# First products, output projection and last norm of a two-layer trunk rearranged between the engines

## Chip, cores and metric

The kernel runs on one core of a Trainium2 chip. The metric is the device time of one execution in microseconds (us), as the median of several runs. The engines are named as in the profile: PE (matmuls), DVE (vector), ACT (activations, casts), POOL, and SP, which issues most loads.

## What is computed

A trunk of two layers on a sequence of T = 1024 tokens with D = 1024 features, batch 1, float32. Layer 0 mixes tokens with a gated linear recurrence (Griffin), layer 1 with a causal pooling mixer; behind each stands an MLP with squared ReLU and 4096 hidden units. Each sub-layer is fed by an RMS norm whose scale and shift come from a conditioning vector c through a large weight matrix (w_mod), and a final RMS norm ends it.

```
for i in range(DEPTH):                         # DEPTH = 2
    mod = silu(c) @ w_mod[i] + b_mod[i]        # 6 columns of D
    sh_m, sc_m, gt_m, sh_f, sc_f, gt_f = split(mod, 6)
    h = rms_norm(x, norm_mix_g[i]) * (1 + sc_m) + sh_m
    y = recurrent_mixer(h, ...) if i == 0 else pool_mixer(h, ...)
    x = x + gt_m * y
    h = rms_norm(x, norm_ffn_g[i]) * (1 + sc_f) + sh_f
    u = relu(h @ ffn_w1[i])
    x = x + gt_f * ((u * u) @ ffn_w2[i])
return rms_norm(x, final_norm_g)

# recurrent_mixer:
#   gate = gelu(h @ w_y + b_y);  xr = conv4(h @ w_in + b_in)
#   r, g = sigmoid(block-diagonal products of xr);  a = exp(c * r * log_sigmoid(lam))
#   s = scan(a, sqrt(1 - a*a) * g * xr);            y = (s * gate) @ w_out + b_out
```

## The kernel before

**Layout.** Everything is kept transposed: features on the 128 partitions in 8 blocks, tokens along the free axis in two halves h = 0 and 1 of 512. x, h and all products are tiles of 128x512.

**Products.** Each float32 product is made of three fp32r matmuls (`mm3`, lines 188 to 190): high part of the weight by high part of the data, high by low, low by high. Eight blocks of features are accumulated, so one output tile takes 24 matmuls. The data are split in `norm_split` (line 291; high part `hh` by ACT, low part `hl` by DVE). A weight of 128x1024 is loaded by SP into a buffer of a pool of three (`rawp`), cast by ACT (line 180) and subtracted by DVE or POOL (line 181), in two halves of 512 (`split_unit`, `split_part`). With "dma" it goes another way (`neg_part`, lines 163 to 165): ACT casts, ACT negates the cast, and a DMA issued by POOL loads the weight a second time and adds it to the negated cast.

**Conditioning.** A column of `mod` is made from eight rows of w_mod: a load of 512 KB into a `rawp` buffer (`mb`) and a DVE multiply with accumulation (line 207). `mod_steps` lists these steps; `drip(n)` puts n of them into the program, and `split_unit` calls it `rate[0]` times behind each weight load. The first two columns (scale and shift of the first norm) are different: their rows `mw` have buffers of their own, and a custom DVE operation (line 333) works on them during the first products.

**First products (lines 316 to 413).** `w_in` for output blocks 0 to 5 and half 0, run with the feature block k on the outside, so that 6 accumulators grow while k proceeds: 18 matmuls (line 410) for each k. For each k, DVE makes the two columns of k (`bias_of`, `scale_of`), xn = x * rstd is made by DVE (k = 0) or POOL (`normed`), ACT makes `hh` and the unsplit value, and DVE the low part. `prepare(q)` splits the weights w_k of q = 0 to 3 (each serves k = 2q and 2q + 1): three casts on ACT, three subtractions on POOL (q = 0: on DVE). `after()` writes out the order of ACT, DVE and POOL by hand here: each call stands behind the one before on its engine.

**Recurrence (lines 565 to 577).** For each of four heads `hd` and each half: `gates` (cast of the conv output into `xchl`, line 516; 24 short matmul steps; sigmoid, exp, tanh, sqrt on ACT; scan on DVE), and two `gelu_block`s with 24 matmuls each. At the end the result is split into `yh`, `yl` (`split_y`, line 558).

**Output projection (lines 586 to 607).** 16 tiles of 24 matmuls, weights w_o0 to 3 for both halves, then 4 to 7. ACT scales (line 602), DVE adds to x (line 603), ACT squares and DVE or POOL adds the square to a sum (`SumSq`, line 243; each letter of the plan names the engine of a step, and each engine of a plan has a part of its own). When half 0 is done and one more tile is under way, `ffn_norm` runs: `rstd_bcast` (line 266) sums each part over partitions with matmuls of one column (line 272), takes root and reciprocal, and spreads the result with two matmuls (line 286).

**MLPs, pooling and end.** The MLP goes in 8 chunks of hidden units (`f1`, `f2`); the first chunk of layer 0 follows the output projection. The last chunk of layer 1 runs half 0, then tokens 0 to 255 and 256 to 511 of half 1 (`last_chunk`), and each is followed by its `final_norm`.

Within the limits of pools and dependencies, the order on an engine is set by a scheduler by priority, in the order in which the program is written, except where `after()` sets it.

## Time and profile before

| | |
|---|---|
| median of 3 runs | 1766.14 us (1762.34 to 1766.17) |
| the profiled execution | 1766.89 us, span 1765.1 us |
| mean granted PE clock | 0.984 of full speed |
| PE / DVE / ACT / POOL busy | 97% / 77% / 54% / 31% of the span |
| DMA over the span | 102 GB/s |

The span is the time from the first to the last record; 1.8 us of the execution lie around it. A busy PE says little alone, since matmuls at a low clock also count as busy. What a stretch loses is seen from PE's waits in it, and from the granted clock: the fraction of full speed, of which there are two levels, 1.2 GHz (0.5) and 2.4 GHz (1.0). DVE, ACT and POOL cost time only where PE waits for them.

### The profile page before, as it was taken

The numbers are of one execution on the slowest core, as the hardware profiler recorded it, in microseconds if no ns is written. First come the engines' busy times: TensorE is split into PE (matmuls) and PEld (weight loads), VectorE is DVE, ScalarE is ACT, GpSimd is POOL, SyncE is SP. The second block draws the span as 40 slices with busy tenths as digits, with TensorE's granted clock in tenths as the row PEclk, the third lists the DMA queues.
The fourth block names the chain that finished last, engine by engine and source line by source line (L and its number), as shares of the span: only waits on it lengthen the run. The fifth ranks groups of instructions, "written<-read, shape, count | busy, mean of one in ns | idle before, by whom it ended". The sixth has DMA issues, their size and how long they took to land.

```text
span 1765.1 us, 20959 instructions
## 1 busy us (share of the span) xinstructions
PE 1704.2 (97%) x7510; PEld 1397.7 (79%) x7510; DVE 1367.9 (77%) x2092; ACT 959.7 (54%) x1648; POOL 544.3 (31%) x442
## 2 busy tenths in 40 slices
PE   5899989989999999999999999999999999999997
PEld 3687768778788888888888888888878787878787
DVE  8898866678888888888874698649786968686836
ACT  4578884346354545444456688745444454545432
POOL 4323332151313223241407433312231404140403
PEclk8999999989999999999999999999999999999998
DMA  9223413521424142423217889861111111111202
GB/s 354 90 72 107 144 60 108 190 84 48 140 71 135 60 143 72 132 73 118 84 48 166 196 182 194 171 167 47 61 37 60 54 42 60 48 61 36 78 7 96
DMA packets 59577, 180.80 MB, mean 102 GB/s; under 512 B 6352, under 2 KB 8784, under 8 KB 59472
## 3 DMA queue, kind: packets, MB, share of 16 engines
q1 hardware_dynamic: 47376, 157.43, 27.7%
q0 software_dynamic: 12096, 22.03, 7.5%
q8 instruction: 59, 0.97, 0.2%
q14 instruction: 46, 0.38, 0.1%
HBM read 175.24 MB, written 4.19 MB: 102 GB/s over the span
## 4 chain that ended last, share of the span: by engine, by line
PE 71%; DVE 15%; ACT 5%; DMA 4%; issue 3%; POOL 1%; SPq 0%; DVEq 0%; ACTq 0%; POOLq 0%
PE mm L188 23%; PE mm L189 23%; PE mm L190 23%; DMA mb<-in_wmod 3%; DVE mb L207 2%; DVE mw L333 1%; DVE xca L449 1%; DVE xa L780 1%; PE sm L272 1%; DVE xb L780 1%; POOL xa L789 1%; DVE xcb L449 1%; DVE hl L301 1%; DVE nt L294 1%; POOL asq L538 1%
## 5 line engine op out<-in xcount | busy, mean ns | idle before, releaser
L188 PE MATMUL mm<-hh,w_w 128*128 128x512 f32 x1024 | 400.3, 391 | 1.0 <-DVE xa L780 1.0
L189 PE MATMUL mm<-hl,w_w 128*128 128x512 f32 x1024 | 399.4, 390 | 0.0
L190 PE MATMUL mm<-hh,w_w 128*128 128x512 f32 x1024 | 399.3, 390 | 0.0
L789 POOL TENSOR_TENSOR xb<-xb,c 128x512 f32<-128x512 f32 x104 | 149.8, 1440 | 603.9 <-ACT c L784 558.9
L188 PEld LDWEIGHTS mm<-hh,w_w 128*128 128x128 f32 x1024 | 192.8, 188 | 42.5 <-DVE xa L780 2.7
L190 PEld LDWEIGHTS mm<-hh,w_w 128*128 128x128 f32 x1024 | 192.8, 188 | 40.4
L189 PEld LDWEIGHTS mm<-hl,w_w 128*128 128x128 f32 x1024 | 192.8, 188 | 39.8
L789 POOL TENSOR_TENSOR xa<-xa,c 128x512 f32<-128x512 f32 x104 | 160.0, 1538 | 145.0 <-ACT c L784 145.0
L784 ACT ACTIVATE c<-c,mod 128x512 f32<-128x512 f32 x104 | 75.3, 724 | 204.5 <-DVE c L810 119.0
L207 DVE SCALAR_TENSOR_TENSOR mb<-mb,cond 128x1024 f32<-128x1024 f32 x80 | 115.3, 1442 | 53.7 <-DMA mb<-in_wmod 53.5
L630 ACT ACTIVATE relu<-mm 128x512 f32<-128x512 f32 x128 | 76.3, 596 | 140.8 <-PE mm L190 140.7
L780 DVE SCALAR_TENSOR_TENSOR xa<-mm,mod,xa 128x512 f32<-128x512 f32 x156 | 113.0, 742 | 25.8 <-POOL xa L789 21.0
L181 DVE TENSOR_TENSOR w_w<-raw_w,w_w 128x512 fp32r<-128x512 f32 x112 | 108.5, 977 | 12.0 <-ACT w_w L180 11.7
L165 POOL DMA_DIRECT2D w_w<-in_w x72 | 63.9, 906 | 106.6 <-ACT w_w L164 65.9
L180 ACT CAST w_w<-raw_w 128x512 fp32r<-128x512 f32 x120 | 69.8, 612 | 27.9 <-PE mm L190 20.6
L620 DVE TENSOR_TENSOR u<-usq,u 128x512 fp32r<-128x512 f32 x102 | 70.3, 689 | 17.1 <-ACT u L619 16.7
L188 PE MATMUL mm<-u,w_a_a 128*128 128x512 f32 x200 | 79.1, 396 | 2.2 <-DVE xa L780 1.0
L188 PE MATMUL mm<-u,w_w 128*128 128x512 f32 (+1 forms) x224 | 81.0, 362 | 0.0
L189 PE MATMUL mm<-u,w_w 128*128 128x512 f32 (+1 forms) x224 | 80.6, 360 | 0.1
L190 PE MATMUL mm<-u,w_w 128*128 128x512 f32 (+1 forms) x224 | 80.4, 359 | 0.0
L189 PE MATMUL mm<-u,w_a_a 128*128 128x512 f32 x200 | 78.0, 390 | 0.0
L190 PE MATMUL mm<-u,w_a_a 128*128 128x512 f32 x200 | 77.9, 389 | 0.0
(336 smaller groups left out, 4113.9 us busy)
## 6 DMA issues: line engine op xcount, KB each, us to landing
raw_w<-in_w SPq DMA_DIRECT2D x148, 512.0 KB, 3.6
mb<-in_wmod SPq DMA_DIRECT2D x80, 512.0 KB, 3.7
w_w<-in_w POOLq DMA_DIRECT2D x72, 256.0 KB, 5.5
mw<-in_wmod SPq DMA_DIRECT2D x16, 512.0 KB, 9.2
raw_in<-in_w_in SPq DMA_DIRECT2D x8, 512.0 KB, 3.6
raw_y<-in_w_y SPq DMA_DIRECT2D x8, 512.0 KB, 3.6
raw_o<-in_w_out SPq DMA_DIRECT2D x8, 512.0 KB, 3.7
outT<-o SPq DMA_DIRECT2D x12, 256.0 KB, 2.3
```

The lines of the kernel that those rows point to most:

```text
L165: nc.gpsimd.dma_start(w[:, 1, 0:n], src, accum_op=ALU.add)
L180: S.copy(w[:, 0, 0:n], raw)
L181: (eng or V).tensor_sub(w[:, 1, 0:n], raw, w[:, 0, 0:n].bitcast(F32))
L188: PE.matmul(out=ps, lhsT=wh, rhs=rh, start=first, stop=False)
L189: PE.matmul(out=ps, lhsT=wh, rhs=rl, start=False, stop=False)
L190: PE.matmul(out=ps, lhsT=w[:, 1, c:c + P], rhs=rh, start=False, stop=last)
L207: V.scalar_tensor_tensor(raw, raw, 1.0, cond, op0=ALU.mult, op1=ALU.mult, accum_out=m[:, e:e + 1])
L620: eng.tensor_sub(u[n][:, 1, jj, :], src, u[n][:, 0, jj, :].bitcast(F32))
L630: S.activation(r, ps, AF.Relu)
L780: V.scalar_tensor_tensor(xb, ps, g[:, r + 4 * row:r + 4 * row + 1], xb, op0=ALU.mult, op1=ALU.add)
L784: S.activation(t, src, AF.Identity, scale=g[:, r + 4 * row:r + 4 * row + 1])
L789: G.tensor_add(xb, xb, t)
```

## The change

1. SP's loads at the start: the rows of w_k for q = 1 to 3 are loaded ahead of the rows mw of e = 3 to 7.
2. First products: all eight xn are made by DVE. POOL's seven multiplies go, and the copy `bc_sb` that they read. The low parts of w_k for q = 1 to 3 (9 tiles) are made by 9 negations on ACT and 9 DMAs that POOL issues, instead of 9 subtractions on POOL; they are prepared at k = 0, 1, 2 instead of 0, 2, 4.
3. Recurrence: `rate` is 0, 1, 2, 3 over the heads instead of 0, 1, 2, 2; the split of half 0 is issued between gates and GeLU blocks of the last head's half 1, the loads of w_o0 to 3 behind the loop.
4. Output projection: the squares of both halves are summed by DVE alone (one part instead of two). `rate` is 0 instead of 4; one drip stands behind each of the first 8 tiles. 26 drips lie ahead of the MLP instead of 31; the others move into its first chunk. w_o4 to 7 take the "dma" way (8 negations, 8 DMAs) instead of DVE subtractions. The first chunk's w1 takes it too instead of POOL subtractions (8 each).
5. `norm_split`: three blocks of eight (k = 1, 3, 5), in the four ffn norms, lose their second ACT operation and their POOL subtraction and get a DVE operation like the others.
6. Two further sums of squares (plans of "n0a" and of the last chunk's half 0) go to DVE alone.
7. The last norm (256 tokens) gets `rstd_row`: two matmuls of a 128x128 block of ones with the two parts, root and reciprocal on 128x256, and the result is read from there. This takes the place of 4 matmul pairs of one column, root and reciprocal on 128x2, a cast, a subtraction, two multiplies of 128x256 and two matmuls.

```diff
@@ -110,7 +110,7 @@
         return part * n, part * n + n
 
     mw = [slot(f"mw{e}", (2, D)) for e in range(NB)]
-    for what in "0w1w23w45w67":
+    for what in "0ww1w2w34567":
         if what == "w":
             q = len(k_raw)
             if q == 0:
@@ -288,15 +288,10 @@
             trace[S], trace[V] = root, last
         return bc
 
-    def norm_split(x, bc, a, b, hh, hl, lean=()):
+    def norm_split(x, bc, a, b, hh, hl):
         for k in range(NB):
             t = tmp("nt")
             V.scalar_tensor_tensor(t, x[:, k, :], a[:, k:k + 1], bc, op0=ALU.mult, op1=ALU.mult)
-            if k in lean:
-                S.activation(t, t, AF.Identity, bias=b[:, k:k + 1])
-                S.copy(hh[:, k, :], t)
-                G.tensor_sub(hl[:, k, :], t, hh[:, k, :].bitcast(F32))
-                continue
             last = (S.activation(hh[:, k, :], t, AF.Identity, bias=b[:, k:k + 1]),
                     V.scalar_tensor_tensor(hl[:, k, :], t, b[:, k:k + 1], hh[:, k, :].bitcast(F32),
                                            op0=ALU.add, op1=ALU.subtract))
@@ -343,7 +338,6 @@
     def scale_of(k):
         column(a, 1, k, vcol("gmix0", k), b1[:, k:k + 1])
 
-    bc_sb = tmp("bc_sb")
     tail_of[V] = last
     scale_of(0)
     bc0 = rstd_bcast(s0, tail_of)
@@ -367,20 +361,17 @@
         split(parts[q][2], c, r2[:, c])
         if q == 0:
             return low
-        for args in low:
-            after(G.tensor_sub, *args)
+        for (dst, _, first), src in zip(low, (w_k[q, :, 0:H], w_k[q, :, H:D], w_k[q, :, D:D + H])):
+            after(S.activation, dst, first, AF.Identity, scale=-1.0)
+            after(G.dma_start, dst, src, accum_op=ALU.add)
 
     xn = {}
 
     def normed(k):
         xn[k] = tmp("xn")
-        if k == 0:
-            after(V.tensor_mul, xn[k], x[0][:, k, :], bc0)
-        else:
-            after(G.tensor_mul, xn[k], x[0][:, k, :], bc_sb)
+        after(V.tensor_mul, xn[k], x[0][:, k, :], bc0)
 
     low = prepare(0)
-    after(S.copy, bc_sb, bc0)
     bias_of(0)
     for k in range(3):
         normed(k)
@@ -400,8 +391,8 @@
         if k == 0:
             for args in prepare(0, 1):
                 after(V.tensor_sub, *args)
-        if k % 2 == 0 and k < 6:
-            prepare(k // 2 + 1)
+        if k < 3:
+            prepare(k + 1)
         if k + 3 < NB:
             normed(k + 3)
         for low, r in ((0, hh), (0, hl), (1, hh)):
@@ -563,17 +554,17 @@
             V.tensor_sub(yl[h][:, k, :], xc[h][:, k, :], yh[h][:, k, :].bitcast(F32))
 
     for hd in range(4):
-        rate[0] = min(hd, 2)
+        rate[0] = hd
         ug = split_unit(w_g[hd], f"g{hd}")
         uy = [split_unit(w_y[m], f"y{m}") for m in (2 * hd, 2 * hd + 1)]
         for h in range(2):
             gates(hd, ug, h)
+            if (hd, h) == (3, 1):
+                split_y(0)
             for mi in range(2):
                 gelu_block(2 * hd + mi, uy[mi], h)
-            if hd == 3:
-                if h == 1:
-                    wo = [split_unit(w_out[m], f"o{m}", G, 0) for m in range(4)]
-                split_y(h)
+    wo = [split_unit(w_out[m], f"o{m}", G, 0) for m in range(4)]
+    split_y(1)
 
     af = [None, None]
 
@@ -583,18 +574,18 @@
             af[i] = norm_scale(vcol(f"gffn{i}"), mod[i, 4], f"affn{i}")
         bc = rstd_bcast(ss)
         new_h(h)
-        norm_split(x[h], bc, af[i], mod[i, 3], hh[h], hl[h], (1, 3, 5))
+        norm_split(x[h], bc, af[i], mod[i, 3], hh[h], hl[h])
 
 
     drip_until(0, 2)
     gtb = const.tile([P, NB], F32, name="gtb")
     V.tensor_mul(gtb, mod[0, 2], vcol("bout"))
     room = slot("ssq")
-    ss = [SumSq("f00", plan="GVGVGVGV", room=room[:, 0:2, :]), SumSq("f01", plan="GVGVGVGV", room=room[:, 2:4, :])]
-    rate[0] = 4
+    ss = [SumSq("f00", plan="VVVVVVVV", room=room[:, 0:1, :]), SumSq("f01", plan="VVVVVVVV", room=room[:, 1:2, :])]
+    rate[0] = 0
     for m0 in (0, 4):
         if m0:
-            wo = [split_unit(w_out[m], f"o{m}") for m in range(m0, m0 + 4)]
+            wo = [split_unit(w_out[m], f"o{m}", "dma") for m in range(m0, m0 + 4)]
         for h in range(2):
             for m in range(m0, m0 + 4):
                 ps = proj(wo[m - m0], yh[h], yl[h])
@@ -602,6 +593,8 @@
                 S.activation(t, ps, AF.Identity, bias=gtb[:, m:m + 1], scale=mod[0, 2][:, m:m + 1])
                 V.tensor_add(x[h][:, m, :], x[h][:, m, :], t)
                 ss[h].add(x[h][:, m, :])
+                if m0 == 0:
+                    drip(1)
                 if h == 1 and m == 4:
                     ffn_norm(0, 0, ss[0])
 
@@ -857,7 +850,7 @@
     def jobs(i, first, last):
 
         for c in range(first, last):
-            yield from f1_jobs(i, c, G if (i, c) == (0, 0) else None)
+            yield from f1_jobs(i, c, "dma" if (i, c) == (0, 0) else None)
             yield from f2_jobs(i, c)
         yield from f1_jobs(i, last)
 
@@ -957,7 +950,7 @@
 
 
 
-    sa, sb = SumSq("n0a", plan="GVGVGVGV"), SumSq("n0b", plan="VVVVVVVV")
+    sa, sb = SumSq("n0a", plan="VVVVVVVV"), SumSq("n0b", plan="VVVVVVVV")
     qa, qb = SumSq("f1a", plan="VVVVVVVV"), SumSq("f1b", plan="VVVVVVVV")
     f1(0, 6, AB, fast=True, ahead=ahead)
     drip_until(1, 5)
@@ -997,6 +990,17 @@
     osrc = outT.rearrange("(b p) t -> p b t", p=P)
     units = [split_unit(w2[1, 7, dp], f"w2_1_7_{dp}") for dp in range(4)]
 
+    def rstd_row(ss):
+
+        parts = list(ss.parts.values())
+        ps = small_ps()[:, 0:ss.n]
+        for pi, a in enumerate(parts):
+            PE.matmul(out=ps, lhsT=ones, rhs=a, start=(pi == 0), stop=(pi == len(parts) - 1))
+        r = tmp("rrow", ss.n)
+        S.activation(r, ps, AF.Sqrt, bias=eps, scale=1.0 / D)
+        V.reciprocal(r, r)
+        return r
+
     def final_norm(bc, h, t0, n):
         per = H // n
         for k0 in range(0, NB, per):
@@ -1028,10 +1032,10 @@
         yield
 
     n1 = 256
-    sa = last_chunk(0, 0, H, "GVGVGVGV")
+    sa = last_chunk(0, 0, H, "VVVVVVVV")
     sb = last_chunk(1, 0, n1, "VVVVVVVV", once(lambda: final_norm(rstd_bcast(sa), 0, 0, H)))
     sc = last_chunk(1, n1, H - n1, "VVVVVVVX", mid_norm())
-    final_norm(rstd_bcast(sc), 1, n1, H - n1)
+    final_norm(rstd_row(sc), 1, n1, H - n1)
 
 
 def _layout(inputs):
```

**Where instructions move.** Names in the rows: `w_k_0`, `w_k_1` and `k_n` are the split weights of the first products, with a number of their own for each q; an ACTIVATE that writes a weight tile from itself is a negation; `xa`, `xb` are the halves of x.

POOL in the first products, before: multiplications of xn and subtractions of w_k alternate.

```order
L330 TENSOR_TENSOR xn<-xa_81,bc_sb 128x512
L333 TENSOR_TENSOR xn<-xa_81,bc_sb 128x512
L333 TENSOR_TENSOR w_k_0_236<-raw_k_107,w_k_0_236 128x512
L333 TENSOR_TENSOR w_k_1_237<-raw_k_107,w_k_1_237 128x512
L333 TENSOR_TENSOR k_0_192<-kr,k_0_192 128x512
```

The change there, from q = 1 on:

```order
L325 DMA w_k_0_234<-in_w_k 128x512
L328 DMA w_k_1_235<-in_w_k 128x512
L328 DMA k_0_192<-in_w_k 128x512
L328 DMA w_k_0_270<-in_w_k 128x512
L328 DMA w_k_1_271<-in_w_k 128x512
```

POOL computes nothing there any more; it issues nine DMAs.

ACT in the same place, the step k = 1 and what is prepared in it, before (two steps lie between two preparations):

```order
L333 ACTIVATE hh_0_182<-xn,mod_0_179,amix_178 128x512
L333 ACTIVATE xn<-xn,mod_0_179,amix_178 128x512
L333 CAST w_k_0_294<-raw_k_114 128x512
L333 CAST w_k_1_295<-raw_k_114 128x512
L333 CAST k_1_193<-kr 128x512
```

The change there:

```order
L328 ACTIVATE hh_0_182<-xn,mod_0_179,amix_178 128x512
L328 ACTIVATE xn<-xn,mod_0_179,amix_178 128x512
L328 CAST w_k_0_270<-raw_k_110 128x512
L328 CAST w_k_1_271<-raw_k_110 128x512
L328 CAST k_1_193<-kr 128x512
L328 ACTIVATE w_k_0_270<-w_k_0_270 128x512
L328 ACTIVATE w_k_1_271<-w_k_1_271 128x512
L328 ACTIVATE k_1_193<-k_1_193 128x512
```

Three negations come behind the three casts, in each of the steps k = 0, 1 and 2.

ACT in the last head (`gate` sigmoid, `a` and the second `gate` exp and tanh, the third root; `xchl` is the split conv output that the gates of the last head's half 1 multiply), before:

```order
L533 ACTIVATE a<-gate,coef 128x512 x2
L534 ACTIVATE gate<-gate,ncoef 128x512 x2
L542 ACT_TABLE_LOAD
L542 ACTIVATE gate<-gate 128x512 x2
L554 ACT_TABLE_LOAD
L554 ACTIVATE gelu<-mm,vec 128x512
L516 CAST xchl<-xcb_471 128x1024
```

The change, with the same cast:

```order
L524 ACTIVATE a<-gate,coef 128x512 x2
L525 ACTIVATE gate<-gate,ncoef 128x512 x2
L507 CAST xchl<-xcb_478 128x1024
L533 ACT_TABLE_LOAD
L533 ACTIVATE gate<-gate 128x512 x2
```

The cast stood behind the root and the first GeLU of the last head's half 0; it now stands two sets of gates earlier, behind the tanh of the head before.

PE at the sum of squares of half 1, in the first MLP chunk (w_w_0_0_0 and w_w_0_0_1 are w1 of the first two tiles), before:

```order
L188 MATMUL mm<-hh_1_2654,w_w_0_0_0_512_2800 128x512
L189 MATMUL mm<-hl_1_2656,w_w_0_0_0_512_2800 128x512
L190 MATMUL mm<-hh_1_2654,w_w_0_0_0_512_2800 128x512
L272 MATMUL sm<-ones,ssq 128x1 x8
L188 MATMUL mm<-hh_0_2653,w_w_0_0_1_0_2810 128x512
```

The change (12 matmuls of w_w_0_0_1's first half stand ahead of the first row):

```order
L188 MATMUL mm<-hh_1_2654,w_w_0_0_1_512_2811 128x512
L272 MATMUL sm<-ones,ssq 128x1 x4
L189 MATMUL mm<-hl_1_2656,w_w_0_0_1_512_2811 128x512
L190 MATMUL mm<-hh_1_2654,w_w_0_0_1_512_2811 128x512
L188 MATMUL mm<-hh_1_2654,w_w_0_0_1_512_2811 128x512
L189 MATMUL mm<-hl_1_2656,w_w_0_0_1_512_2811 128x512
L190 MATMUL mm<-hh_1_2654,w_w_0_0_1_512_2811 128x512
L188 MATMUL mm<-hh_1_2654,w_w_0_0_1_512_2811 128x512
L189 MATMUL mm<-hl_1_2656,w_w_0_0_1_512_2811 128x512
L286 MATMUL sm<-dg,ones_r 128x512
```

The sum has half the matmuls and stands 13 matmuls later; 7 stand between it and the first of the two that spread the result, where 11 stood. At the sum of half 0 its place is the same, with 4 instead of 8, and 16 matmuls stand between it and the spread in both.

## Rows read from the trace of the kernel before

**Rows 1.** Waits of PE, at 20 to 69 us: us in total, times, longest.

```profile
PE mm L410 <- DVE hl L333: 5.0, 5, 1.8
PE mm L410 <- ACT hh L333: 3.7, 2, 2.2
PE mm L188 <- ACT xr L435: 2.7, 1, 2.7
```

**Rows 2.** The same at 237 to 276 us, then at 340 to 395 us.

```profile
PE mm L188 <- ACT xchl L516: 5.7, 1, 5.7
PE mm L188 <- ACT gelu L554: 0.8, 1, 0.8
...
PE sm L272 <- POOL ssq L263: 4.9, 2, 2.7
PE sm L272 <- DVE ssq L263: 3.4, 2, 1.9
```

**Rows 3.** Stretches: length, busy us (instructions) of PE, PEld, DVE, ACT, POOL; PEclk, DMA, GB/s.

```profile
22.00:44.00 22.00, 17.19 (x62) 12.40 (x62) 21.47 (x21) 7.86 (x12) 16.30 (x10) 0.85 0.95 365
1000.00:1060.00 60.00, 60.00 (x269) 49.74 (x269) 56.87 (x102) 51.01 (x104) 20.47 (x22) 1.00 0.80 173
275.00:340.00 65.00, 65.00 (x288) 53.85 (x287) 42.81 (x65) 21.29 (x36) 11.05 (x7) 1.00 0.54 177
257.00:275.00 18.00, 17.64 (x70) 14.45 (x71) 9.60 (x13) 16.36 (x24) 7.19 (x6) 0.89 0.09 30
353.00:376.00 23.00, 23.00 (x94) 18.79 (x95) 18.84 (x23) 13.11 (x23) 16.39 (x10) 0.92 0.28 92
```

**Rows 4.** Instructions of the first products' weights: ns min/median/max, first and last start.

```profile
L410 PE MATMUL mm<-hh,w_k x64: 389/389/794, 20.2 to 65.1; 128*128 128x512 f32 x64
L333 ACT CAST w_k<-raw_k x6: 603/610/617, 15.2 to 36.4; 128x512 fp32r<-128x512 f32 x6
```

**Rows 5.** Timeline of DVE in the first products: start, us, instruction.

```profile
30.15 2.28 DVE L333 CUSTOM_DVE_ANT_0 mw<-mw,cond,bmix 128x1024 f32<-128x1024 f32 x1
...
32.36 0.68 DVE L333 TENSOR_TENSOR hl<-xn,hh 128x512 fp32r<-128x512 f32 x1
32.96 1.27 DVE L333 CUSTOM_DVE_ANT_0 mw<-mw,cond,vec 128x1024 f32<-128x1024 f32 x1
```

**Rows 6.** Timeline of POOL at 29 to 36 us, all there is.

```profile
27.68 3.67 POOL L333 TENSOR_TENSOR xn<-xa,bc_sb 128x512 f32<-128x512 f32 x2
```

**Rows 7.** ACT groups at 20 to 66 us: busy us, mean ns, idle before.

```profile
L333 ACT ACTIVATE hh<-xn,mod,amix 128x512 fp32r<-128x512 f32 x8 | 6.5, 815 | 24.4 <-DVE mod L333 23.6 <-DVE xn L333 0.8
```

**Rows 8.** The page's third part, DMA queues: packets, MB, share of 16 engines' span.

```profile
q1 hardware_dynamic: 47376, 157.43, 27.7%
q0 software_dynamic: 12096, 22.03, 7.5%
```

**Rows 9.** Line 165, the accumulating DMAs of the whole run: issue (ns), landing.

```profile
L165 POOL DMA_DIRECT2D w_w<-in_w x72: 852/872/1667, 938.7 to 1165.9; - x72
...
DMA to landing us min/median/max: 3.8/5.6/8.3
```

**Rows 10.** Line 165 at 1000 to 1060 us alone: landing.

```profile
DMA to landing us min/median/max: 4.0/5.7/7.3
```

**Rows 11.** Timeline around the first sum of squares, DVE, then PE.

```profile
343.89 1.23 DVE L207 SCALAR_TENSOR_TENSOR mb<-mb,cond 128x1024 f32<-128x1024 f32 x1 [2.06 <-DMA mb<-in_wmod]
...
349.79 3.14 PE L272 MATMUL sm<-ones,ssq 128*128 128x1 f32 x14 [1.56 <-DVE ssq L263]
```

**Rows 12.** Timeline of PE behind the second sum of squares.

```profile
385.60 0.63 PE L189 MATMUL mm<-hl,w_w 128*128 128x512 f32 x1
...
389.87 0.63 PE L286 MATMUL sm<-dg,ones_r 128*128 128x512 f32 x1
```

**Rows 13.** Timeline of the end, PE and DVE.

```profile
1755.25 0.38 PE L272 MATMUL sm<-ones,ssqo1256X 128*128 128x1 f32 x2 [0.52 <-ACT ssqo1256X L258]
...
1758.38 3.22 DVE L1005 SCALAR_TENSOR_TENSOR o<-xb,vec,sm 128x256 f32<-128x256 f32 x8 [0.73 <-issue]
```

## The prediction

> **What bounds the kernel now.** I read PE's waits first, then the stretches with the granted clock, then the timelines at the waits. In a long undisturbed stretch PE is busy all the time: 288 matmuls in 65.00 us at full clock [rows 3], 0.226 us each. PE is the bound, so a change can gain only where PE waits or runs at the low clock. The places that the change touches hold most of such loss. In the first products PE waits 8.7 us for DVE's low parts and ACT's high parts [rows 1]; DVE is busy 21.47 of 22 us beside it, POOL 16.30, and the DMA engines 0.95 [rows 3]. In the last head PE waits 5.7 us for one cast that ACT does late, and 0.8 us for a GeLU [rows 2]. At the two sums of squares it waits 4.9 us for POOL's part and 3.4 us for DVE's [rows 2]. Behind the longer waits the clock is low: 0.89 over the 18 us from 257 us, 0.92 over the 23 us from 353 us [rows 3], and behind the second sum ten matmuls take 4.27 us, 0.427 each instead of 0.226 [rows 12]: this is the level of 1.2 GHz. What the reader is to see is that each wait has one late predecessor, and that the low clock behind it adds about a third of the wait.
>
> **First products.** For each k, PE needs 18 matmuls: 4.1 us at full clock, 7.7 us at the low one. The custom operation on a column takes 2.28 us in one row and 1.27 in the next but one [rows 5]; POOL multiplies from 27.68 to 31.35 us [rows 6], during the first and not during the second. With POOL's arithmetic gone I take 1.27 for both columns of k. DVE then has 2 x 1.27, a low part of 0.68 [rows 5], and xn, which is new to it for k = 1 to 7 and bounded by the same 0.68 from below and the 1.27 from above; I take 0.68, being the same shape. That is 3.9 us, under PE's 4.1. ACT has two operations of 0.815 [rows 7] for each k, and for k = 0, 1, 2 three casts of 0.61 [rows 4] and three negations. No negation stands in these rows; between the cast's 0.61 and 0.815 I take 0.61, a copy being nearest: 5.3 us for such a k. The first matmul is at 20.2 us, some take 794 ns where the median is 389 [rows 4], and the clock of the stretch is 0.85 [rows 3]: the first k is at the low clock, and its 7.7 us cover ACT. New waits: 2 x (5.3 - 4.1) = 2.4 us at k = 1 and 2. The stage loses 8.7 us of waits and gains 2.4: **-6.3**.
>
> The low parts now come by DMA. Those of q = 1 are needed 12 matmuls into k = 2: 20.2 + 7.7 + 5.3 + 2.7 = 35.9 us. ACT has negated them some 5.4 us into k = 0, at about 25.6; one issue takes 0.87 us, and landing 3.8 to 8.3 us [rows 9], so they are there at 30.3 to 34.8. Cover is 1 us at the long end. In this stretch the queues are full, which line 165 never met at 0.95; nothing bounds the landing from above but the load itself. Per MB the software queue takes 7.5/22.03 against 27.7/157.43 for the other [rows 8], 1.93 times the time: 9 x 0.262 MB count as 4.6 MB, 12.5 us at 365 GB/s. The bound is then: loads that end near 44 us end near 56.5, and the last rows of w_mod, needed for k = 7 one step ahead near 51 us, are 5.5 us late, which leaves -0.8. I keep -6.3, since DVE and ACT use the rows one k at a time, and -0.8 for the range.
>
> POOL's issue stands beside a busy DVE elsewhere: at 1000 to 1060 us DVE is busy 56.87 of 60 us [rows 3], and line 165 lands in 4.0 to 7.3 us there, 5.7 in the median, against 5.6 over all [rows 9, 10]. The Trainium skill speaks against this edit: "DMA: Bandwidth & Descriptors", section "SWDGE vs HWDGE vs iDMA", says that POOL writes the descriptors of its DMAs into on-chip memory out of which DVE locks it in its two-port mode, and "GPSIMD Engine Reference", section "Specifications", counts DVE instructions with two SBUF inputs as contending too. By the row this term stays -6.3; by the rule it is the rival worked out below.
>
> SP's new order costs nothing by itself: the rows mw3 to mw7 come later by the 2.1 MB of w_k pulled ahead of them, and are needed last.
>
> **Last head.** The late cast now stands behind the tanh of the head before, with its source long done. The 5.7 us and the 0.8 us go, and with them the low clock: (1 - 0.89) x 18 = 2.0 us. **-8.5**. What may be late next is a GeLU or a gate, since three drips per weight instead of two stand in DVE's queue there: one costs 1.23 us, after 2.06 us of waiting for its load in the worst row [rows 11]. If one such pair reaches PE, 3.3 come back. Bounds -5.2 and -9.
>
> **Sums of squares.** With one part on DVE the chain from the last tile is two ACT operations (0.815) and two DVE operations (0.68), 3.0 us. The sum of half 0 follows one more tile: 24 x 0.226 = 5.4 us. The sum of half 1 follows 24 + 13 matmuls, 8.4 us. What made the chain late was the drips between the additions: DVE stood 2.06 us for a load and then worked 1.23 us [rows 11]. They no longer stand there (rate 0). So the 8.3 us of waits go. Half the one-column matmuls go too: 14 of 16 take 3.14 us [rows 11]; eight at the full clock take 0.9 (an estimate, 3.14 x 8/14 halved), which saves 2 x 2.2 = 4.4 us. The low clock goes: (1 - 0.92) x 23 = 1.8 us, and at the second place 12 matmuls at 0.2, 2.4 us. New: only 7 matmuls (1.6 us) now cover root, reciprocal and the rest up to the spread at the second sum; from the last such matmul to the use of the result it is 3.1 us at the end of the kernel [rows 13], and I charge 1.0. Together **-15.9**; if half of the waits and of the low clock stays, -8. Work that is moved for this: w_o4 to 7 by DMA. Their buffers come free when half 1 has used w_o0 to 3, three tiles (16.3 us) before each is needed; casts, negations and issues take some 2.5 us and landing up to 8.3, so 5.5 us stay. The first drips stand behind tiles with 5.4 us of PE each, and 26 of them are more than the 25 that `ffn_norm` needs.
>
> **MLP chunk, norms.** Five drips move behind the sums: 5 x 1.23 = 6.2 us more for DVE, which at 353 to 376 us is idle 4.2 of 23 us [rows 3]; the chunk is longer than that, and POOL's subtractions of w1, which stretch DVE's operations as above, are gone from it. I take +0.5, bounds 0 and +2. Six low parts of `norm_split` in the first two norms go to DVE, in the same idle time. The plans of the later sums cost nothing: PE waits for none of them now.
>
> **Last norm.** From the first one-column matmul that needs ACT's last square to the output multiply it is 3.13 us [rows 13]. Now: two matmuls with 256 columns. Float32 with that shape is not in the rows: at least the 0.38 of the one-column form, at most twice the low-clock time of a row of 512, 0.85. Root 0.4 to 0.8, reciprocal 0.34 (half of 0.68) to 1.3 (twice a DVE operation of 512 columns at 0.68), and some 0.6 for three hand-overs. 2.1 to 4.4 us; I take 2.6, as the first sort of row is nearest in shape: **-0.5**, bounds -1.0 and +1.3.
>
> **Sum.** -6.3 - 8.5 - 15.9 + 0.5 - 0.5 = -30.7. The profiled execution took 1766.9 us, 0.75 above the median of the runs: 1736.2, or 1735.5 from the median. I say **1736**.
>
> **Rivals.**
> - *The sums, or the cast, still come late* (a gate, a GeLU or an addition behind the drips that are left): half of -15.9 and 3.3 of the last head come back, 1736 + 8 + 3.3 = 1747. For it: DVE stays full at the first, and three drips per weight stand in the last head. Against it: rate 0 at the additions. 0.15.
> - *DMA bounds the first products*, as worked out: 1736 + 5.5 = 1742. For it: 0.95 [rows 3] with 4.6 MB more to carry. 0.12.
> - *DVE holds back POOL's DMAs.* The low parts of q = 1 land only when DVE has run through its first products, 20.2 + 8 x 4.4 = 55 us, plus 3.8: near 59 instead of 35.9. PE then has six k to go, 24.4 us and some 3 at the low clock, and ends near 86 instead of 66 us: +20 where -6.3 was counted, 1762. The landing times beside a busy DVE speak against it [rows 9, 10]. 0.05. It is the case in which that rule of the Trainium skill holds.
> - *Slower.* DVE's fixed order turns into a convoy: a drip's multiply waits for a load whose buffer (three for weights and drips together) another engine still holds, and the gates behind it wait, as the late cast did. Each time costs PE what that cast cost, 5.7 + 0.8 + 2.0 = 8.5 us. There are now nine drips in the last head and eight in the projection. The gain is gone from four such stalls on (34 us): 1770; five give 1779. Against it: before, 16 drips in the projection's second part made one such wait that PE saw. 0.06.
>
> **How the numbers follow.** The forecast has 0.62. Its own bounds run from -34 to about -20 when two terms fall short together, 1733 to 1747. The range takes in the first two rivals and a little beyond both ends: 1727 to 1753. Left out are the last two rivals and tails of the first. A measurement here tells 0.3%, 5.3 us, from no change. Faster: forecast, first two rivals, 0.88 with tails taken off. Same: the DMAs held back and part of the convoy, 0.06. Slower: the convoy, 0.06.
>
> **What would show it.** Right: the last matmul of line 410 near 59 us, and DVE's custom operation at 1.3 us throughout; no wait for `xchl` in the last head; waits at line 272 near zero at the two sums and the clock at 1.0 around them; landing of w_k under 10 us. Wrong: PE waiting in line 410 for POOL's DMAs or for mw; a DVE row of a drip with a long wait for its load ahead of a gate; a new low stretch of the clock in the projection, at w_o4 above all; a reciprocal over 1.3 us at the end.

## The result, and the profile after

The changed kernel takes 1740.76 us (median of 4 runs, 1740.37 to 1741.31) where the kernel before took 1764.88 beside it (4 runs, 1762.34 to 1766.17): a ratio of 0.9868, with a 95% interval of 0.9853 to 0.9884. That is 1.3% faster. The forecast was 1736, the range 1727 to 1753. The profiled execution took 1740.37 us, 26.5 less than the profiled one before; its span is 1738.5 us, 26.6 less. The two traces therefore differ by 2.4 us more than the medians (24.1), mostly since the profiled run before lay above its median.

Where the 26.6 us went is read by taking the same instruction in both traces and subtracting its start. Each row is a place in the program; the last column is what the stretch up to it gained (differences are taken before rounding).

| first (or last) instruction | before, us | after, us | gained so far | in the stretch |
|---|---|---|---|---|
| last matmul of the first products | 65.6 | 57.4 | 8.2 | 8.2 |
| first gates | 130.0 | 122.8 | 7.2 | -0.9 |
| gates of the last head, half 0 | 232.0 | 225.8 | 6.2 | -1.1 |
| output projection | 274.8 | 262.3 | 12.5 | 6.3 |
| second product of the first MLP chunk | 426.3 | 401.4 | 24.9 | 12.4 |
| second product of the seventh chunk | 922.0 | 897.8 | 24.2 | -0.7 |
| last matmul of the last MLP | 1752.8 | 1726.6 | 26.2 | 2.1 |
| end | 1765.1 | 1738.5 | 26.6 | 0.3 |

PE's waits in the changed kernel, at 15 to 66 us, then at 225 to 260 and at 345 to 400 (us in total, times, longest), answer to [rows 1, 2]:

```profile
PE mm L188 <- ACT xr L426: 4.0, 1, 4.0
PE mm L401 <- DMA k<-in_w_k: 2.1, 2, 1.6
PE mm L401 <- ACT hh L328: 1.9, 1, 1.9
PE sm L286 <- DVE dg L284: 1.7, 1, 1.7
PE mm L401 <- DVE hl L328: 0.2, 1, 0.2
...
PE mm L188 <- ACT gelu L545: 1.9, 1, 1.9
...
PE sm L272 <- DVE mod L210: 3.9, 1, 3.9
```

In the first products the 8.7 us for DVE and ACT have shrunk to 2.1, and a wait for POOL's DMAs has come, 2.1 us. Of the 2.1 us for DVE and ACT, 1.9 are the wait for the very first `hh`; that wait was there before too, as 2.2 of the 8.7 us. The wait behind them, for `xr`, has grown from 2.7 to 4.0. In the last head the cast is gone from the list, and the GeLU has grown from 0.8 to 1.9. Of the sums, the first has no wait; the second still has 3.9.

Stretches of the changed kernel (columns as in [rows 3]: length, busy us of PE, PEld, DVE, ACT and POOL, granted clock, DMA share, GB/s):

```profile
22.00:44.00 22.00, 20.27 (x82) 15.13 (x82) 18.81 (x31) 15.58 (x25) 7.19 (x8) 1.00 1.07 326
230.00:250.00 20.00, 18.13 (x73) 14.49 (x72) 14.53 (x20) 19.23 (x28) 6.68 (x5) 0.91 0.22 82
340.00:353.00 13.00, 13.00 (x59) 10.76 (x58) 12.75 (x21) 12.28 (x21) 4.05 (x6) 1.00 0.97 210
353.00:376.00 23.00, 19.06 (x81) 15.48 (x80) 16.83 (x33) 8.31 (x14) 0.51 (x1) 0.93 0.49 145
```

At 22 to 44 us DVE is no longer full (18.81 of 22), but the DMA engines are, and they move fewer bytes for it: 326 GB/s where it was 365. The clock is low in two of the four, behind the GeLU and behind the second sum; it is also low at 60 to 80 us (0.83), behind the wait for `xr`.

DVE's custom operation in the whole first stage (ns min/median/max, first and last start), which took 2.28 and 1.27 in [rows 5]:

```profile
L328 DVE CUSTOM_DVE_ANT_0 mw<-mw,cond,bmix x8: 1339/1342/1345, 11.8 to 47.2; 128x1024 f32<-128x1024 f32 x8
L328 DVE CUSTOM_DVE_ANT_0 mw<-mw,cond,vec x8: 1278/1280/1285, 15.9 to 49.3; 128x1024 f32<-128x1024 f32 x8
```

All sixteen are short: POOL computes nothing there any more. The loads of x's half 1, in the changed kernel and then in the kernel before (issue in ns, then landing in us):

```profile
L95 SPq DMA_DIRECT2D xb<-in_xT x4: 368/379/1541, 39.4 to 47.2; - x4
...
DMA to landing us min/median/max: 12.8/14.7/16.6
```

```profile
L95 SPq DMA_DIRECT2D xb<-in_xT x4: 427/464/637, 40.5 to 42.0; - x4
...
DMA to landing us min/median/max: 5.6/6.9/9.8
```

They are there at 55.9 to 60.0 us, where before it was 46.2 to 51.8. With POOL's nine DMAs taken out again and all else as changed (the second experiment below) they are there at 43.4 to 47.4, so the DMAs are what delays them. ACT stands in front of their squares, and `xr`, which is to empty the accumulators for PE, stands behind the squares.

DVE in the changed kernel at the second sum (start, us, instruction, idle before and what ended it):

```profile
358.83 1.23 DVE L207 SCALAR_TENSOR_TENSOR mb<-mb,cond 128x1024 f32<-128x1024 f32 x1 [2.08 <-DMA mb<-in_wmod]
359.99 0.08 DVE L207 DVE_READ_ACCUMULATOR mb<-mb,cond 128x1 f32 x1
359.99 0.69 DVE L594 TENSOR_TENSOR xb<-xb,wo 128x512 f32<-128x512 f32 x1
361.26 1.23 DVE L207 SCALAR_TENSOR_TENSOR mb<-mb,cond 128x1024 f32<-128x1024 f32 x1 [0.59 <-DMA mb<-in_wmod]
362.41 0.08 DVE L207 DVE_READ_ACCUMULATOR mb<-mb,cond 128x1 f32 x1
362.41 0.69 DVE L263 TENSOR_TENSOR ssq<-ssq,sq 128x512 f32<-128x512 f32 x1
```

The last tile's product was scaled by 355.6 us; its addition to x runs at 359.99, behind a drip that waited 2.08 us for its load, and the last addition to the sum stands behind a second one. PE's one-column matmuls start at 363.24. The drips that the prediction took away from the sums are still there: they belong to w1 of the first MLP chunk.

### The profile page after: what moved, and what is told of

Read it like the earlier page. It is cut to its first block, busy times and chain, and to the rows that moved or that the text cites. A ratio compares the mean times of both kernels' runs of the same rounds, so it can differ in the third digit from the quotient of the medians.

```text
span 1738.5 us, 20871 instructions
## 1 busy us (share of the span) xinstructions
PE 1690.5 (97%) x7472; PEld 1386.7 (80%) x7472; DVE 1358.9 (78%) x2115; ACT 967.2 (56%) x1660; POOL 492.3 (28%) x419
## 4 chain that ended last, share of the span: by engine, by line
PE 75%; DVE 10%; issue 3%; ACT 3%; DMA 2%; POOL 1%; DVEq 0%; ACTq 0%; POOLq 0%
PE mm L188 25%; PE mm L189 25%; PE mm L190 25%; DMA mb<-in_wmod 2%; DVE mb L207 1%; DVE xa L773 1%; DVE xb L773 1%; POOL xa L782 1%; DVE xcb L440 1%; DVE w_a_s L181 1%; ACT c L777 0%; DVE gate L530 0%; PE sm L272 0%; DVE w_y L181 0%; DVE w_s L181 0%
## 5 line engine op out<-in xcount | busy, mean ns | idle before, releaser
L181 DVE TENSOR_TENSOR w_w<-raw_w,w_w 128x512 fp32r<-128x512 f32 x112 | 106.8, 962 | 12.4 <-ACT w_w L180 12.4
L165 POOL DMA_DIRECT2D w_w<-in_w x80 | 70.5, 900 | 151.0 <-ACT w_w L164 120.6
L180 ACT CAST w_w<-raw_w 128x512 fp32r<-128x512 f32 x112 | 65.1, 612 | 25.0 <-PE mm L190 17.3
```

Source lines behind the costliest of these rows:

```text
L165: nc.gpsimd.dma_start(w[:, 1, 0:n], src, accum_op=ALU.add)
L180: S.copy(w[:, 0, 0:n], raw)
L181: (eng or V).tensor_sub(w[:, 1, 0:n], raw, w[:, 0, 0:n].bitcast(F32))
```

## Experiments

All are edits of the changed kernel. Times are single executions where no range is given; the changed kernel is at 1740.4 to 1741.3. Line numbers in waits are those of each kernel.

How far single executions can be told apart is seen at the projection. Six of the kernels below have their edits behind it: shared sums, the drips of the projection, w_o4 to 7, no drips ahead of the second sum, and the two with moved drips. Up to the projection they run the same instructions as the changed kernel, in the same order on every engine. They start it at 259.8 to 263.1 us, the changed kernel at 262.3. The earliest, the kernel with shared sums, is 2.5 us ahead, and 1.8 of this is the clock: behind the same GeLU wait of about 2 us it fell in the changed kernel (0.91 above) and stayed up here:

```profile
230.00:250.00 20.00, 18.02 (x80) 14.60 (x79) 14.52 (x21) 19.85 (x29) 6.90 (x6) 1.00 0.20 71
```

A difference of some 3 us between two totals therefore says little by itself. Where it matters, times are also counted from the start of the projection in the same trace.

**The first products as before.** The load order, `normed`, `prepare` and their calls are those of the kernel before.

```diff
-    for what in "0ww1w2w34567":
+    for what in "0w1w23w45w67":
...
-            after(S.activation, dst, first, AF.Identity, scale=-1.0)
-            after(G.dma_start, dst, src, accum_op=ALU.add)
...
+            after(G.tensor_sub, *args)
...
-        if k < 3:
-            prepare(k + 1)
+        if k % 2 == 0 and k < 6:
+            prepare(k // 2 + 1)
```

> The changed kernel with the first products as before (loads, xn on POOL, subtractions on POOL, preparation at k = 0, 2, 4). Theory A: the first products are worth what the two traces differ by at the first gates, 7.2 us, and all of it passes to the end, since DVE's work behind them moves with PE: 1747.6, between 1746 and 1749. Theory F (another bound behind them, the GeLU or DVE in the chunks, takes back part of it): 1742 to 1745.

Measured 1747.7 us. The first gates are at 129.0 us (6.2 later), the projection at 268.2 (5.9 later), the last matmul 7.7 later. The stage is worth 6 to 7.7 us, and nothing of it is taken back on the way to the end. Theory F falls.

**Only the low parts by POOL's subtraction.**

```diff
-        for (dst, _, first), src in zip(low, (w_k[q, :, 0:H], w_k[q, :, H:D], w_k[q, :, D:D + H])):
-            after(S.activation, dst, first, AF.Identity, scale=-1.0)
-            after(G.dma_start, dst, src, accum_op=ALU.add)
+        for args in low:
+            after(G.tensor_sub, *args)
```

> The changed kernel with the low parts of w_k for q = 1 to 3 subtracted by POOL again, all else as changed (xn on DVE, order of the loads, preparation at k = 0, 1, 2). Theory A (POOL's arithmetic stretches DVE's operations from 1.3 to 2.3 us, and this is what the DMAs buy off): the last of the first products ends 2 to 5 us later than the 57.4 us of the changed kernel, partly made up by x of half 1 landing in time: 1742 to 1745. Theory G (the DMAs cost as much by filling the queues, x of half 1 landing 8 us late, as they save): 1739 to 1741.

Measured 1742.18 us. The first products end at 61.7 us, 4.3 later, as theory A has it; but x of half 1 lands in 9.5 to 10.5 us, the wait for `xr` is 2.1 instead of 4.0, and at the first gates 2.0 us are left, at the end 1.7. Two of DVE's custom operations take 2.30 us again, each beside POOL's subtractions. So the DMAs save 4.3 us and give 2.3 of them back through the queues: both theories name a real cost. A's total only just holds, and the two totals lie too near each other to be told apart by one execution. At the first gates the whole stage is worth 6.2 us and the DMAs 2.0; the other 4.2 come from xn on DVE, the early preparation and the order of the loads, which were not taken apart.

**x of half 1 loaded first.** `load_x(1)` stands behind the loop over mw, and the squares of half 1 ahead of the casts of w_in6 and 7.

```diff
+    load_x(1)
     ident = const.tile([P, P], F32, name="ident")
...
+    s1 = SumSq("m01", plan="VVVVVVVV")
+    for k in range(NB):
+        s1.add(x[1][:, k, :])
     uin = {m: split_unit(w_in[m], f"in{m}") for m in (6, 7)}
-    load_x(1)
...
-    s1 = SumSq("m01", plan="VVVVVVVV")
-    for k in range(NB):
-        s1.add(x[1][:, k, :])
```

> The changed kernel with the loads of x's half 1 ahead of those of w_in6 and later, and its squares ahead of the casts of w_in6 and 7. What was learned: with two accumulators drained early PE started 3.7 us earlier and then stood 7.3 us for the norm of half 1. Theory A (what ends last behind the first products is the chain from x of half 1, whose loads the accumulating DMAs delay): x lands at 47 to 56 us instead of 52 to 61, the waits of 1 and 0.6 us at 75 to 78 us go, the first gates come at 119 to 121.3 instead of 122.8, and all of it passes to the end: 1737 to 1739.5. Rival (the queue is full until 60 us whatever the order, and the weights w_in6 and 7 are late by what x gains): gates at 122 to 125, 1740 to 1743.

Measured 1738.8 us (5 runs, 1737.25 to 1740.01; ratio to the kernel before beside it 0.9850, interval 0.9836 to 0.9863). PE continues 1.5 us earlier behind the first products, but then waits 2.2 us for `hh` of half 1: the first gates come at 122.1, where the rival has them, and not at 119 to 121.3. x of half 1 is there at 51.6 to 56.0 us, 4 us earlier. The projection starts 3.0 us earlier and the last matmul 1.7 earlier; but only 0.6 of the 3.0 are there at the first gates, and behind the GeLU the clock of this execution stayed at 1.00. So the total is the one theory A expected, and the way to it is not. The intervals of the two ratios overlap: it is the fastest kernel of the study by some 2 us, not one that is proved faster than the change.

**The issue order of the last head as before.** `split_y(0)` behind the GeLU blocks of half 0, the loads of w_o0 to 3 ahead of `split_y(1)` inside the loop; three drips stay.

```diff
-            if (hd, h) == (3, 1):
-                split_y(0)
             for mi in range(2):
                 gelu_block(2 * hd + mi, uy[mi], h)
-    wo = [split_unit(w_out[m], f"o{m}", G, 0) for m in range(4)]
-    split_y(1)
+            if hd == 3:
+                if h == 1:
+                    wo = [split_unit(w_out[m], f"o{m}", G, 0) for m in range(4)]
+                split_y(h)
```

> The changed kernel with the split of half 0 and the loads of w_o0 to 3 issued where they were before; three drips per weight in the last head as changed. Theory A (issuing the split of half 0 later is what let ACT make the cast for the last gates early; the third drip does no harm): the wait of PE for that cast comes back, 5 to 6 us, with a low clock behind it of about 2 us less the 1.8 that the change has anyway: the projection starts at 268 to 270 us instead of 262.3, total 1746 to 1748. Theory H (the drips set the place of the cast): no wait for the cast, 1740 to 1742.

Measured 1749.55 us; the projection starts at 270.2 us, 7.9 later. PE's waits at 225 to 345 us:

```profile
PE mm L188 <- ACT xchl L507: 4.8, 1, 4.8
PE mm L188 <- ACT gelu L545: 2.2, 1, 2.2
PE mm L189 <- DVE xchl L508: 0.5, 1, 0.5
```

The cast's wait is back, with three drips per weight as it was with two; ACT's order has the cast behind the first GeLU again. Theory A stands: the order of issue, not the drips, moved the cast. The time lies 1.6 us above its range; 1.0 more came behind the second sum. Which of the two moved calls did it, the split of half 0 or the loads of w_o0 to 3, was not tried apart.

**The sums shared by POOL and DVE again.**

```diff
-SumSq("f00", plan="VVVVVVVV", room=room[:, 0:1, :])
+SumSq("f00", plan="GVGVGVGV", room=room[:, 0:2, :])
```

(and f01 alike.)

> The changed kernel with the sums of squares at the output projection shared by POOL and DVE again, as before. Theory A (drips, not POOL's part, made the sums late): twice the one-column matmuls cost 0.9 us at each sum, the first sum stays covered by the tile ahead of it, the second waits 0.5 to 1.5 us longer: 1743, between 1742 and 1745. Theory B (POOL's part, an addition of 1.3 to 2.3 us instead of 0.7, is what made them late): both waits come back with the low clock behind them, 1749 or more.

Measured 1741.94 us. The first sum waits 1.9 us (1.6 of it for DVE), the second 1.4 instead of 3.9. POOL's part is not most of what made the sums late: the two waits are 3.3 us together, where the kernel before had 8.3. The total hides what it costs, since this execution started the projection 2.5 us earlier than the changed kernel, with the edit still to come. Counted from there, the second product of the first chunk comes 3.3 us later. That is within what theory A's range means (1 to 4 us), though theory A had the first sum covered, and far from theory B (8 or more).

**The drips of the projection as before.**

```diff
-    rate[0] = 0
+    rate[0] = 4
...
-                if m0 == 0:
-                    drip(1)
```

> The changed kernel with the drips of the projection as before: four behind each weight of the second part, none behind the first eight tiles. Theory A (drips between the additions hold up the sums): PE waits 2 to 4 us at the first sum and the clock falls behind it, 1745 to 1749. Theory B: with DVE alone on the sums the drips do no harm, 1740 to 1742.

Measured 1759.71 us, far above either figure. PE's waits at 225 to 345 us, and behind them:

```profile
PE mm L190 <- DMA w_o<-in_w_out: 7.5, 3, 7.0
PE mm L188 <- ACT gelu L545: 1.9, 1, 1.9
PE mm L188 <- ACT w_o L163: 1.7, 1, 1.7
...
PE sm L272 <- DVE ssq L263: 7.5, 2, 3.9
```

The wait at the sums is there, as theory A has it. But the larger part is new: the loads of w_o4 to 7 stand behind four drips each in the three buffers (SP issues four loads of drips at 310.2 to 318.2 us and one weight at 318.3, where the changed kernel issues all four weights at 288.8 to 298.1), and with the accumulating DMA behind load, cast and negation they come too late for PE. The kernel before had the same drips with DVE's subtraction and no wait for w_o. Here the drips and the "dma" way did not go together; the change had to move the one to afford the other.

**w_o4 to 7 by DVE's subtraction.**

```diff
-            wo = [split_unit(w_out[m], f"o{m}", "dma") for m in range(m0, m0 + 4)]
+            wo = [split_unit(w_out[m], f"o{m}") for m in range(m0, m0 + 4)]
```

> The changed kernel with w_o4 to 7 split by DVE subtractions again instead of negation and DMA. Theory A (only what waits for loads holds up the sums; eight subtractions of 0.7 to 1.0 us fit beside them): 1740 to 1742, no wait at the first sum. Theory C (taking DVE work away from the additions is what made the first sum punctual): a wait of 2 us or more at the first sum, and 1743 to 1747.

Measured 1743.64 us. There is no wait at the first sum, so theory C falls; but theory A's time fails too. Of the 2.9 us, 0.65 were there at the start of the projection, ahead of the edit. The second sum starts 1.0 us later than in the changed kernel, the first chunk's second product 2.5 and the third chunk's 3.4. That eight subtractions more on DVE (8 x 0.69 us) cost PE there fits this; one execution does not prove it.

**No drips ahead of the second sum.** The four that go with w1 of the first chunk stand behind the tiles that follow the sum.

```diff
...
-split_unit(w1[i, c * 4 + j], f"w1_{i}_{c}_{j}", eng, DRIPS[j])
+split_unit(w1[i, c * 4 + j], f"w1_{i}_{c}_{j}", eng, 0 if (i, c) == (0, 0) else DRIPS[j])
...
+    def first_side():
+        ffn_norm(0, 1, ss[1])
+        yield
+        for _ in range(4):
+            drip(1)
+            yield
...
-    f1(0, 0, AB, by_half=True, side=once(lambda: ffn_norm(0, 1, ss[1])), fast="in turn", ahead=ahead)
+    f1(0, 0, AB, by_half=True, side=first_side(), fast="in turn", ahead=ahead)
```

> The changed kernel, but the four drips that go with w1 of the first MLP chunk stand behind the second sum of squares, one behind each of the tiles that follow it. Theory A (what still holds up the second sum is DVE working on drips, and standing for their loads, ahead of the last additions): the wait at the one-column matmuls falls from 3.9 us to under 0.5, the low clock behind it (1.6 us) goes too, and the moved drips cost up to 1 us in the chunk: 1735.5, between 1734.5 and 1737. Theory B (the chain of additions is too long by itself, or DVE's work only moves and comes back in the chunk): 1740 to 1741.

Measured 1741.86 us: no gain. The wait at the sum is gone and its matmuls start at 357.3 instead of 363.2, so theory A is right on the cause. Of these 5.9 us 2.7 are no gain: the sum's matmuls stand 12 places earlier in PE's order. At the second product 3.1 us are left (3.9 counted from the projection) of the 5.5 that the wait and the low clock had cost, and at the end of the next chunk none. 1.3 us went to a new wait for `dg`, ahead of the matmuls that spread the result: the one for which the prediction charged 1.0. PE's waits from 355 to 860 us, without those drips and then in the changed kernel:

```profile
PE mm L188 <- DVE xa L773: 3.3, 4, 1.2
PE mm L188 <- DVE xb L773: 1.8, 4, 0.7
PE sm L286 <- DVE dg L284: 1.3, 1, 1.3
PE mm L189 <- DVE ut L613: 0.4, 1, 0.4
```

```profile
PE sm L272 <- DVE mod L210: 3.9, 1, 3.9
PE mm L188 <- DVE xa L773: 1.9, 2, 1.0
PE mm L188 <- DVE xb L773: 1.2, 5, 0.4
```

And the stretch from 402 to 442 us, in the same order (DVE's busy time is the third figure, of 40 us):

```profile
402.00:442.00 40.00, 38.30 (x163) 29.61 (x162) 37.96 (x58) 16.89 (x30) 20.16 (x14) 1.00 0.29 93
```

```profile
402.00:442.00 40.00, 38.41 (x167) 30.53 (x165) 37.54 (x55) 17.40 (x32) 18.73 (x13) 1.00 0.33 104
```

DVE is nearly full there in both, and PE's waits for DVE come to about 7 us in both lists. The work that made PE wait at the sum makes it wait later: up to 442 us DVE is the second bound.

**Drips taken out of that stretch.** The next two kernels move twelve drips (second products of the first chunk, all of the second chunk) behind the sixth chunk; the first keeps the drips ahead of the second sum, the second does not (its `first_side` is that of the kernel above).

```diff
...
-split_unit(w1[i, c * 4 + j], f"w1_{i}_{c}_{j}", eng, DRIPS[j])
+split_unit(w1[i, c * 4 + j], f"w1_{i}_{c}_{j}", eng, 0 if (i, c) == (0, 1) else DRIPS[j])
...
-        drip(DRIPS[4 + r])
+        drip(0 if (i, c) in ((0, 0), (0, 1)) else DRIPS[4 + r])
...
-    drip_until(1, 5)
+    drip_until(1, 2)
```

> The changed kernel with twelve drips, those of the second products of the first MLP chunk and of the whole second chunk, moved behind the sixth chunk, where DVE is busy 26 of 65 us. What was learned: with the wait at the second sum taken away, all of the gain was given back in the two chunks behind it, where DVE worked at the same instants as without. Theory D (DVE is the second bound from the sums to about 525 us): the 3.1 us of waits for DVE in the chunks go, the 3.9 us at the second sum stay: 1737.5, between 1736.5 and 1739. Theory E (the waits in the chunks come from a single late addition of POOL or from the order, not from the amount of DVE work): 1740 to 1741.5.

> The same, and the drips of the first chunk's w1 stand behind the second sum as in the run without drips ahead of it. Theory D: with DVE no longer at its limit the 5.5 us gained at the second sum stay gained: 1733, between 1731.5 and 1735. Theory E: the gain is given back again, 1738 to 1741.

Measured 1764.09 and 1763.42 us. Up to 442 us both do what theory D says, 3.7 and 4.8 us ahead of the changed kernel (2.5 and 4.5 counted from the projection), where the kernel above had 2.4 (3.2). In the second chunk theory D does not hold: its eight drips are gone, and DVE is busy 64.77 of 83 us in the first of the two where the changed kernel has 71.58, yet PE waits 2.0 us for DVE's additions to x instead of 1.2, and 1.8 and 3.0 us of the lead are left at 525 us. There the order of DVE's work or a late addition (theory E) is not ruled out. And where the drips went, behind 924 us, PE loses 24 us. Its waits at 940 to 1000 us, in the first of the two:

```profile
PE mm L188 <- ACT u L612: 7.4, 2, 6.4
PE sm L272 <- DVE ssqn0aV L263: 5.2, 1, 5.2
PE mm L189 <- DVE u L613: 4.2, 2, 3.9
```

The place was chosen by DVE's free time alone, and it was wrong. The figure for it (busy 26.28 of 65 us) is that of the kernel before; in the changed kernel, where DVE makes the sum "n0a" alone, it is 36.18 of 65 us at 924 to 989 us. But DVE's work is not what stood in the way: with the drips DVE is busy 38.65 of 76 us from 924 us on, and among its own waits there is this one, which the changed kernel does not have:

```profile
DVE mb L207 <- DMA mb<-in_wmod: 22.9, 8, 5.8
```

DVE's order has the drips ahead of the operations that PE waits for, and DVE stands 22.9 us for the loads of the drips. The DMA engines are 0.90 busy in the stretch; whether these loads waited for them or for free buffers was not tried.

**Spread instead, and accumulators drained early.** Two edits at places that the trace tells apart: four drips out of the first chunk, one more in each of chunks 3 to 6 (with the `first_side` of above); and `xr` 0 and 1 ahead of the squares of half 1.

```diff
...
-split_unit(w1[i, c * 4 + j], f"w1_{i}_{c}_{j}", eng, DRIPS[j])
+split_unit(w1[i, c * 4 + j], f"w1_{i}_{c}_{j}", eng, 0 if (i, c) == (0, 0) else 2 if (i, j) == (0, 0) and 2 <= c <= 5 else DRIPS[j])
...
-        drip(DRIPS[4 + r])
+        drip(0 if (i, c) == (0, 0) else DRIPS[4 + r])
...
+    xr = [conv_input(m, ps6[m], 0) for m in range(2)]
+    taken = last_traced(S)
+    with tc.issue_after(taken):
+        for k in range(NB):
+            s1.add(x[1][:, k, :])
...
+    xr += [conv_input(m, ps6[m], 0) for m in range(2, 6)]
```

> The changed kernel with two edits at places that the trace tells apart. First, ACT drains two of the accumulators of the first products before the squares of half 1, which wait for loads, instead of behind them. Theory A (PE's 4.0 us wait behind the first products is for ACT standing in front of x of half 1): w_in's next matmul comes 3 us earlier, at 58.5 to 59.5 instead of 61.8, and the 3 us pass to the end as those of the first products did; the rival is that the sum of squares of half 1 comes later by as much and PE waits there: nothing at the first gates (122.8). Second, no drips ahead of the second sum and none with the second products of the first chunk; the four left over go one each to chunks 3 to 6, ahead of the stretch where moved drips cost 24 us. Theory D (DVE's load in the first chunk is what took the gain back): of the 5.9 us gained at the second sum 3 or more are left at the end of the chunk (442 us). Rival E: less than 1.5 left. Total 1733.5 to 1736 if both hold, 1737 to 1738 with one, 1740 to 1742 with none.

Measured 1743.5 us. PE goes on at 58.1 us, 3.7 earlier, and then stands 7.3 us for `hh` of half 1: the first gates come 1.4 us later than in the changed kernel, so the rival holds. Counted from the projection on, the second sum is 6.7 us ahead (2.7 of it by its earlier place in PE's order), and 3.1 are left at 442 us, just what theory D asked for; at 525 us it is 2.1. But each of the four chunks with one drip more takes 1.1 to 2.1 us longer (PE waits 6.6 us for `xa` at 500 to 860 us), and the end comes 3.1 us later than in the changed kernel. The time is above all three that were expected. In these four chunks a ninth drip cost PE about what a drip takes of DVE, 1.2 us or more.

## Why the prediction was right, and where not

**First products, -6.3: right in size, partly by luck.** The stage gained 7.2 up to the first gates, and undoing it cost 6.9. DVE's custom operations are short throughout, as said. But the terms are not the ones that were added up. The last matmul comes 8.2 us earlier: 1.6 because the first one does (18.7 us instead of 20.2), which was not foreseen; 4.2 by waits behind the first matmul, 6.5 before and 2.3 now; and the remaining 2.4 for the most part by fewer matmuls at the low clock, which had been given no term here. The 8.7 us that were to go include 2.2 for the very first `hh`, and that wait stays, as 1.9. The 2.4 us that were to come for ACT at k = 1 and 2 did not come: ACT takes 4.7 us for such a k (24.53 to 29.23 us), not 5.3. SP's new order was misread too: mw6 and mw7 have the same loads ahead of them as before, and mw4 and mw5 only those of q = 3 more; this cost little. The step that failed is the landing of the low parts, taken as 3.8 to 8.3 us from rows of a less busy stretch [rows 9]. Here it is this (POOL's three other tiles first, then the tile `k`):

```profile
DMA to landing us min/median/max: 7.5/8.1/9.7
...
DMA to landing us min/median/max: 7.1/8.7/11.8
```

The cover of 1 us was not enough: PE waits 1.6 us at q = 1 and 0.5 at q = 2. The bound by the queues' load (1.93 times the time per MB [rows 8]) pointed the right way, only the victim was another: not the rows of w_mod, for which DVE waits 1.26 us once, but x of half 1.

**DVE holding back POOL's DMAs** did not come: the low parts of q = 1 landed 7.9 to 11.8 us after issue, while DVE was busy 18.81 of 22 us, and not at the end of DVE's work. The Trainium skill ("DMA: Bandwidth & Descriptors", section "SWDGE vs HWDGE vs iDMA") says that DVE, in its two-port mode, locks POOL out of the memory in which it writes the descriptors. In this trace no such hold set the time; which mode DVE's operations had here, the profile does not tell.

**Last head, -8.5: 6.3.** The cast moved and its wait went, 5.7 us. The 0.8 for a GeLU and the low clock behind it were counted as gone as well; they stayed, as 1.9 us and (1 - 0.91) x 20 = 1.8 us. The bounds had -5.2 for one such case. The 1.8 us are chance in part: other executions had the same GeLU wait without the low clock.

**Sums, -15.9: 12.4.** The first sum is as said: no wait, full clock. The step that failed is "They no longer stand there (rate 0)". `rate` is not the only source of drips: each weight of the MLP chunk brings one of its own (`DRIPS`), the chunk is started before the last tiles of the projection are added, and DVE's order puts them between. This leaves 3.9 us of wait and (1 - 0.93) x 23 = 1.6 us of low clock. The case without those drips shows the cause, and that the 5.5 us did not stay gained even so: 1.3 went to the spread, and the rest was lost to waits for DVE by the end of the next chunk. 15.9 less 5.5 would be 10.4; of the 2.0 us that came on top, 1.0 is the wait ahead of the spread that had been charged and did not come (at the low clock the 7 matmuls ahead of it took 3.0 us), and the rest is not accounted for.

**MLP chunk, +0.5: 0.7 up to the seventh chunk.** Right in size; but the reason given, DVE's idle time, does not hold between 402 and 442 us, where DVE is busy 37.54 of 40.

**Later sums, 0: about -1.7.** Nothing waited for them, so they were counted as nothing. But PE itself runs the one-column matmuls: eight records fewer at each of the two sums took 0.8 and 0.9 us out of the bound engine.

**Last norm, -0.5: -0.3.** From the last matmul of the MLP to the end it is 12.0 us where it was 12.3. Between the first matmul that needs the last square and the output multiply nearly nothing changed, 3.03 us for 3.13 [rows 13]:

```profile
1728.45 0.70 PE L998 MATMUL sm<-ssqo1256X,ones 128*128 128x256 f32 x2 [0.20 <-ACT ssqo1256X L258]
1729.18 0.47 ACT L1000 ACTIVATE rrow<-sm,eps 128x256 f32<-128x256 f32 x1 [0.79 <-PE sm L998]
1729.69 1.75 DVE L1001 RECIPROCAL rrow<-rrow 128x256 f32<-128x256 f32 x1 [1.80 <-ACT rrow L1000]
1731.48 3.26 DVE L1009 SCALAR_TENSOR_TENSOR o<-xb,vec,rrow 128x256 f32<-128x256 f32 x8
```

Matmuls and root are cheap, and the reciprocal costs 1.75 us, above the bound of 1.3: it was bounded by an addition of 512 columns, and it is no such operation.

**The rivals.** The second sum coming late, from the first rival, is the largest single thing that kept the result from the forecast; the rest of the way is misses in both directions that nearly cancel, so that 1736 was nearer than its terms. The convoy, which was to make the change slower, did not come in the changed kernel. The kernels with the old drips and with the moved ones (1759.7 and 1764) show two things of its kind, 19 and 24 us: weights that come late behind drips, and DVE standing 22.9 us for the loads of drips. What the change of `norm_split` and the move of w1 to the "dma" way are worth alone was not tried.

## What to carry to other kernels

Price a wait that is to be removed by what the engine behind it does next: where the second engine is nearly full in the stretch that follows (here 365 to 442 us, DVE busy over 90%), work that moved out of the wait comes back there. Work taken off that engine kept its gain up to the end of the stretch, but in no kernel here up to the end of the program. Look at what the engine stands for, too, and not only at its free time, before moving loads and their work to another place. A small load that shares its buffers with weights delays those weights; look for all sources of such loads, and not only for the one that the change sets to zero. An engine on the bound is paid for every instruction, so halving small matmuls there counts even where nobody waits. And know how far two executions of the same instructions differ before reading a difference of 2 us.
